# Gate products and whole token-tile splits moved from GpSimd to VectorE at the end of each sub-layer

## Chip, cores and metric

The kernel runs on one core of a Trainium2 chip. The metric is device time in microseconds (us) for one launch. The engines are called PE (TensorE), DVE (VectorE), ACT (ScalarE), POOL (GpSimd) and SP (SyncE, which issues the DMAs).

## What is computed

A trunk of two layers over 256 context tokens and 512 latent tokens of width 1024, in float32. Each layer is a half-step feed-forward block, a token mixer (differential attention in layer 0, grouped-query attention in layer 1), and another half-step feed-forward block. Each of these sub-layers reads a normalised, modulated copy of the residual stream and ends in a gated residual:

```python
def modulated_norm(h, g, m, k):
    return rmsnorm(h, g) * (1.0 + m[..., k + 1, :]) + m[..., k, :]

def gated_residual(h, y, g, m, k, weight):
    return h + weight * m[..., k + 2, :] * rmsnorm(y, g)

# per layer
h = half_ffn(h, m, 0, ...)           # sub-layer s = 0
h = gated_residual(h, mixer(modulated_norm(h, g[2], m, 3)), g[3], m, 3, 1.0)   # s = 1
h = half_ffn(h, m, 6, ...)           # s = 2
```

So between two sub-layers every token tile goes through the same chain: the last partial product of y, the gate product, the mean square of y, the new h, the mean square of h, the normalised h, a transpose, the modulation and a split of the result into a high and a low part for the next sub-layer's matmuls.

## The kernel before

Tokens lie in six tiles of 128 (tiles 0 and 1 context, 2 to 5 latent). Weights and activations are each split into a rounded high part and the remainder, so every product takes three matmuls. The six sub-layers run one after the other; (l, s) below is layer l, sub-layer s. The layer-0 mixer is (0,1), the layer-1 mixer is (1,1), and the other four are feed-forward blocks. The last, (1,2), writes the output and has nothing after it.

In a feed-forward block the output projection is summed over groups of weight rows. In the last group (`w_out_last`) PE goes through the tiles in order, two halves of 512 columns each (`project_half`, matmuls at L423). Each half is added to y by DVE (`add_y`, L414). As soon as both halves of a tile are there the class `Finish` takes the tile through its chain:

- `gated` (L364 to L371, the operation recorded at L369): yg = y * gate for one half of 512 columns, on POOL. The gate rows g were loaded once per sub-layer (`load_gate`, L327). yg is taken from a pool of two buffers in the feed-forward blocks and from the weight buffers wh and wl in the mixers.
- `sumsq` on ACT (L267), then `rms` on POOL, which is two instructions on one column (L97 and L99).
- h = yg * rms + h on DVE (L382, SCALAR_TENSOR_TENSOR over 1024 columns), and a DMA that stores h.
- `sumsq` of h on ACT and `rms` on POOL again, then y = h * rms on DVE (L388, TENSOR_SCALAR over 1024 columns).
- eight transposes on PE into PSUM (`turn`, L280), and the modulation out of PSUM, four blocks on DVE (L294) and four on ACT (L290) in most tiles.
- `split_u`: ACT copies the high part into uh (L310) and the remainder goes into ul. A tile in `WIDE` (thirteen tiles in all: four each at the ends of the sub-layers (0,0), (0,2) and (1,0), one at (0,1)) is split whole: one ACT copy of 1024 columns, then DVE takes the first 512 columns of the remainder (L315) and POOL the other 512 (L316). The other tiles are split in two parts, both remainders on DVE (L318).

Within `w_out_last` of a feed-forward block the order on DVE, ACT and POOL is the program's (a manual schedule). After each half of a tile, the function `stages` advances the tiles that are in flight in the order of stages 3, 4, 5, 1, 2. For DVE that makes, after the first half of a tile t+1: the addition, the modulation of tile t-1, the normalisation (L388) of tile t. After the second half of a tile t: the addition, the remainder of tile t-2, the new h (L382) of tile t. PE's order there, and all orders in the two mixers and at the beginning of the next sub-layer, come from the planner that places instructions by estimated times. The chain of the last two tiles runs on into the next sub-layer, which calls `need(t)` before it uses a tile.

Of the kernel before, what the change touches and what calls it, by code (L numbers as in the profile page):

```python
# [13 lines left out]
ALU = mybir.AluOpType  # L14
# [7 lines left out]
KC = D // P  # L22
# [32 lines left out]
def raw(ap):  # L55
    return ap.bitcast(F32)
# [3 lines left out]
def trunk(ctx: ExitStack, tc: tile.TileContext, a: dict, out: bass.AP):  # L60
    nc = tc.nc
# [85 lines left out]
    marks = {}  # L147
# [155 lines left out]
    def split_u(t, place, parts):  # L303
        i, j = place
        u32 = ys[t].rearrange("p (k q) -> p k q", k=KC)
        n = KC // parts
        for k in range(0, KC, n):
            ks = slice(k, k + n)
            hi, lo = (x[:, i, ks, j * P : (j + 1) * P] for x in (uh, ul))
            marks["act"] = nc.scalar.copy(hi, u32[:, ks])  # L310
            if parts == 1:
                yield
            if parts == 1:
                m = KC // 2
                marks["dve"] = nc.vector.tensor_tensor(out=lo[:, :m], in0=u32[:, :m], in1=raw(hi[:, :m]), op=ALU.subtract)  # L315
                marks["pool"] = nc.gpsimd.tensor_tensor(out=lo[:, m:], in0=u32[:, m:], in1=raw(hi[:, m:]), op=ALU.subtract)  # L316
            else:
                marks["dve"] = nc.vector.tensor_tensor(out=lo, in0=u32[:, ks], in1=raw(hi), op=ALU.subtract)  # L318

    def load_gate(l, s):  # L320
        g = []
# [31 lines left out]
    class Finish:  # L353
# [10 lines left out]
        def gated(self, t, dh):  # L364

            if dh == 0:
                self.yg = self.tile()
            cols = slice(512 * dh, 512 * dh + 512)
            nc.gpsimd.tensor_tensor(  # L369
                out=self.yg[:, cols], in0=ys[t][:, cols], in1=self.gate[1 if t < CT else 0][:, cols], op=ALU.mult  # L370
            )  # L371

        def chain(self, t):
            i, j = self.place[t]
            cols = slice(j * P, (j + 1) * P)
            h = load_h(t, self.first, self.tile if self.s == 1 else None)
            ss = sumsq(ys[t], uh[:, i, :, cols])
            self.gated(t, 1)
            yg = self.yg
            r = rms(ss)  # L380
            yield
            nc.vector.scalar_tensor_tensor(out=h, in0=yg, scalar=r, in1=h, op0=ALU.mult, op1=ALU.add)  # L382
            nc.sync.dma_start(out=hd[t] if self.nxt else out[0, (t - CT) * P : (t - CT + 1) * P], in_=h)
            if not self.nxt:
                return
            r = rms(sumsq(h, ys[t]))
            yield
            nc.vector.tensor_scalar(out=ys[t], in0=h, scalar1=r, scalar2=None, op0=ALU.mult)  # L388
            yield
            pts = turn(t, t in self.wide)  # L390
            modulate(*self.nxt, t, [pts[k // 4][:, (k % 4) * P : (k % 4 + 1) * P] for k in range(KC)])
            yield
            yield from split_u(t, self.place[t], 1 if t in self.wide else 2)
# [1365 lines left out]
```

## Time and profile before

| | |
|---|---|
| median of three runs | 2739.59 us (2735.0 to 2741.33) |
| the profiled execution, whole | 2744.38 us |
| its span, first to last instruction | 2742.6 us |
| granted TensorE clock, mean | 0.988 |
| PE busy | 2639.0 us (96%) |
| DVE busy | 2016.4 us (74%) |
| ACT busy | 1135.7 us (41%) |
| POOL busy | 357.6 us (13%) |

The profile is of one execution. Times are counted from its first instruction. "Busy" is the time between the start and the end of an engine's instructions; consecutive instructions of DVE overlap by some 0.08 us at their ends, so that the spacing of two starts is a little under the duration of the first. A wait is given to the engine whose result came last.

### The profile page before, as it was taken

What the parts mean: (1) busy time and instruction counts of PE and PEld (TensorE: products, weight loads), DVE (VectorE), ACT (ScalarE), POOL (GpSimd) and SP (SyncE); (2) the same over time, 40 slices, a digit from 0 to 9 for tenths busy, and PEclk for the clock granted to TensorE, in tenths of its full rate; (3) what the DMA queues carried; (4) which work ended last, traced back from release to release, by engine and by line L of the source; (5) the groups of instructions that cost most, each with busy time, mean ns of one, the idle gap of its engine ahead of it and who ended that gap; (6) DMA issues with size and microseconds to landing.
All of it is one profiled execution on the core that took longest, in us unless ns stands there. A gap on an engine that the chain in (4) does not pass through costs nothing.

```text
span 2742.6 us, 38868 instructions
## 1 busy us (share of the span) xinstructions
PE 2639.0 (96%) x14720; PEld 2404.6 (88%) x14720; DVE 2016.4 (74%) x3052; ACT 1135.7 (41%) x2323; POOL 357.6 (13%) x643
## 2 busy tenths in 40 slices
PE   6999999989999998999999999999999999899998
PEld 5999998879999987999988789999787899788887
DVE  4988879867777787888788689787766778733355
ACT  4333333156666665333342353333324554622232
POOL 0000000054333343000000310000004210200001
PEclk9999999999999999999999999999999999999999
DMA  7444457531111113444375334344743211444452
GB/s 229 136 132 151 142 170 254 167 122 45 38 32 49 54 63 97 134 124 139 117 251 175 123 104 154 125 137 155 282 141 131 79 39 39 149 142 139 149 166 89
DMA packets 301860, 354.13 MB, mean 129 GB/s; under 512 B 15808, under 2 KB 234088, under 8 KB 301672
## 3 DMA queue, kind: packets, MB, share of 16 engines
q1 hardware_dynamic: 301672, 351.64, 39.9%
q8 instruction: 116, 1.90, 0.3%
q14 instruction: 72, 0.59, 0.1%
HBM read 303.05 MB, written 48.54 MB: 128 GB/s over the span
## 4 chain that ended last, share of the span: by engine, by line
PE 75%; DVE 9%; ACT 5%; issue 5%; POOL 3%; DMA 2%; POOLq 0%; DVEq 0%; ACTq 0%; SPq 0%
PE y_ps L423 23%; PE ff_p L615 15%; PE ff_ps L615 12%; PE ff_ps L735 8%; PE qkv_ps L806 5%; PE ff_ps L477 2%; PE ff_ps L767 1%; DVE h L382 1%; PE S L984 1%; DVE wl L104 1%; PE o_ps L1056 1%; ACT y L267 1%; PE kv_ps L806 1%; PE q_ps L806 1%; PE o_ps L1428 1%
## 5 line engine op out<-in xcount | busy, mean ns | idle before, releaser
L423 PE MATMUL y_ps<-wh,gx 128*128 128x512 f32 x1936 | 604.5, 391 | 1.5 <-ACT wh L103 1.5
L423 PEld LDWEIGHTS y_ps<-wh,gx 128*128 128x128 f32 x1936 | 363.2, 188 | 81.1 <-ACT wh L103 2.9
L103 ACT CAST wh<-stage 128x1024 fp32r<-128x1024 f32 x224 | 232.1, 1048 | 434.7 <-PE y_ps L423 217.0
L423 PE MATMUL y_ps<-wl,gx 128*128 128x512 f32 x968 | 377.3, 390 | 0.5 <-DVE wl L104 0.4
L104 DVE TENSOR_TENSOR wl<-stage,wh 128x1024 fp32r<-128x1024 f32 x224 | 273.2, 1224 | 96.3 <-ACT wh L103 94.4
L414 DVE TENSOR_TENSOR y<-y_ps,y 128x512 f32<-128x512 f32 x324 | 221.3, 686 | 109.3 <-PE y_ps L423 107.7
L369 POOL TENSOR_TENSOR yg<-y,g 128x512 f32<-128x512 f32 x44 | 58.3, 1326 | 1820.3 <-DVE y L414 1818.1
L185 DVE SCALAR_TENSOR_TENSOR acc<-stage,scond,acc 128x1024 f32<-128x1024 f32 x196 | 244.1, 1277 | 30.3 <-DMA stage<-in_ada_w 30.2
L615 PE MATMUL ff_p<-t,wh 128*128 128x384 f32 x960 | 244.4, 335 | 1.5 <-ACT sil L568 1.5
L103 ACT CAST wh<-raw 128x1024 fp32r<-128x1024 f32 x120 | 120.1, 1049 | 255.9 <-DVE raw L594 255.9
L423 PEld LDWEIGHTS y_ps<-wl,gx 128*128 128x128 f32 x968 | 181.8, 188 | 38.5 <-DVE wl L104 1.6
L615 PEld LDWEIGHTS ff_p<-t,wh 128*128 128x128 f32 x960 | 173.8, 188 | 1.8 <-ACT sil L568 1.8
L615 PE MATMUL ff_p<-t,wl 128*128 128x384 f32 x480 | 161.0, 335 | 2.9 <-DVE wl L104 2.9
L615 PE MATMUL ff_ps<-uh,wh 128*128 128x384 f32 x480 | 160.9, 335 | 1.7 <-DVE two L637 1.7
L615 PE MATMUL ff_ps<-uh,wl 128*128 128x384 f32 x480 | 160.4, 334 | 0.0
L615 PE MATMUL ff_ps<-ul,wh 128*128 128x384 f32 x480 | 160.3, 334 | 0.0
L104 DVE TENSOR_TENSOR wl<-raw,wh 128x1024 fp32r<-128x1024 f32 x120 | 141.2, 1218 | 0.0
L806 PE MATMUL qkv_ps<-wh,uh 128*128 128x384 f32 x384 | 136.9, 357 | 4.1 <-ACT wh L849 2.7
L806 PE MATMUL qkv_ps<-wl,uh 128*128 128x384 f32 x384 | 129.8, 338 | 2.5 <-DVE wl L852 2.5
L615 PE MATMUL ff_p<-uh,u 128*128 128x384 f32 x480 | 132.1, 336 | 0.0
L806 PE MATMUL qkv_ps<-wh,ul 128*128 128x384 f32 x384 | 129.9, 338 | 0.1
L615 PE MATMUL ff_ps<-t,wh 128*128 128x384 f32 x480 | 124.6, 340 | 2.2 <-ACT one L633 1.9
(250 smaller groups left out, 6356.4 us busy)
## 6 DMA issues: line engine op xcount, KB each, us to landing
stage<-in_ffn_w_in SPq DMA_DIRECT2D x176, 512.0 KB
stage<-in_ada_w SPq DMA_DIRECT2D x136, 512.0 KB
stage<-in_ffn_w_out SPq DMA_DIRECT2D x88, 512.0 KB
gd<-g SPq DMA_DIRECT2D x66, 384.0 KB
gr<-gd SPq DMA_DIRECT2D x57, 384.0 KB
stage<-in_da_w_in SPq DMA_DIRECT2D x64, 192.0 KB
hd<-h SPq DMA_DIRECT2D x18, 512.0 KB
h<-hd SPq DMA_DIRECT2D x16, 512.0 KB
```

The lines of the kernel that those rows point to most:

```text
L103: nc.scalar.copy(hi, src)
L104: nc.vector.tensor_tensor(out=lo, in0=src, in1=raw(hi), op=ALU.subtract)
L185: nc.vector.scalar_tensor_tensor(out=acc[c], in0=st, scalar=scond[:, k, c : c + 1], in1=acc[c], op0=ALU.mult, op1=ALU.add)
L267: nc.scalar.activation(junk, src, AF.Square, accum_out=ss)
L369: nc.gpsimd.tensor_tensor(out=self.yg[:, cols], in0=ys[t][:, cols], in1=self.gate[1 if t < CT else 0][:, cols], op=ALU.mult)
L382: nc.vector.scalar_tensor_tensor(out=h, in0=yg, scalar=r, in1=h, op0=ALU.mult, op1=ALU.add)
L414: nc.vector.tensor_tensor(out=y, in0=ps, in1=y, op=ALU.add)
L423: nc.tensor.matmul(ps, lhsT=x, rhs=w, start=(i == 0), stop=(i == n - 1))
L477: nc.tensor.matmul(ps, lhsT=ww[:, k, :], rhs=moving(uu, k, two), start=(k == 0 and n == 0), stop=(k == KC - 1 and n == 2),)
L615: nc.tensor.matmul(ps[:, :hw], lhsT=ww[:, k * P : (k + 1) * P], rhs=bb[:, k, cols], start=(first and k == 0 and n == 0), stop=(last and k ...
L735: nc.tensor.matmul(ps[:, :nt], lhsT=ww[:, k, :], rhs=uu[:, :, k, cols], start=(k == 0 and n == 0), stop=(k == KC - 1 and n == 2),)
L806: nc.tensor.matmul(ps[:, :n], lhsT=x, rhs=w, start=(k == 0 and m == 0), stop=(k == KC - 1 and m == 2))
```

## The change

Both edits move work from POOL to DVE. The gate product is issued on DVE at the same place of the program, all 64 of them. The remainder of a whole split is one DVE instruction of 1024 columns in place of two of 512 on two engines. POOL keeps the two one-column instructions of `rms` for each mean square. The dictionary `marks`, which holds the last instructions behind which the next feed-forward block places its first weight loads, no longer gets an entry for POOL from the split; `rms` still sets one.

```diff
@@ split_u
             marks["act"] = nc.scalar.copy(hi, u32[:, ks])
             if parts == 1:
                 yield
-            if parts == 1:
-                m = KC // 2
-                marks["dve"] = nc.vector.tensor_tensor(out=lo[:, :m], in0=u32[:, :m], in1=raw(hi[:, :m]), op=ALU.subtract)
-                marks["pool"] = nc.gpsimd.tensor_tensor(out=lo[:, m:], in0=u32[:, m:], in1=raw(hi[:, m:]), op=ALU.subtract)
-            else:
-                marks["dve"] = nc.vector.tensor_tensor(out=lo, in0=u32[:, ks], in1=raw(hi), op=ALU.subtract)
+            marks["dve"] = nc.vector.tensor_tensor(out=lo, in0=u32[:, ks], in1=raw(hi), op=ALU.subtract)
@@ Finish.gated
             cols = slice(512 * dh, 512 * dh + 512)
-            nc.gpsimd.tensor_tensor(
+            nc.vector.tensor_tensor(
                 out=self.yg[:, cols], in0=ys[t][:, cols], in1=self.gate[1 if t < CT else 0][:, cols], op=ALU.mult
             )
```

## Rows read from the trace of the kernel before

**Rows 1.** Five ends, stretches: busy (count) of PE, PEld, DVE, ACT, POOL; clock; DMA

```profile
540.00:606.00 66.00, 56.37 (x267) 47.85 (x266) 43.95 (x57) 31.33 (x62) 35.30 (x44) 0.95 0.43 139
983.00:1072.00 89.00, 71.11 (x391) 60.34 (x390) 73.51 (x127) 58.45 (x147) 42.23 (x66) 0.90 0.27 90
1538.00:1606.00 68.00, 61.59 (x342) 53.05 (x341) 45.70 (x61) 32.10 (x61) 31.72 (x40) 0.97 0.33 109
2066.00:2136.00 70.00, 60.04 (x305) 51.92 (x304) 47.73 (x65) 31.46 (x63) 36.98 (x46) 0.90 0.45 143
2336.00:2386.00 50.00, 40.48 (x250) 35.38 (x249) 38.23 (x56) 32.63 (x67) 19.50 (x24) 0.93 0.37 123
```

**Rows 2.** PE's waits at the end of (0,2): total us, times, longest

```profile
PE pre_t L280 <- DVE y L388: 2.8, 3, 1.7
PE ff_ps L477 <- ACT y L290: 1.9, 1, 1.9
PE ff_ps L477 <- DVE wl L104: 1.0, 1, 1.0
```

**Rows 3.** PE's waits at the end of (0,0)

```profile
PE qkv_ps L806 <- ACT wh L849: 2.7, 1, 2.7
PE qkv_ps L806 <- DVE wl L852: 2.5, 1, 2.5
PE pre_t L280 <- DVE y L388: 2.3, 2, 1.7
PE k_t L934 <- POOL ks L927: 2.1, 1, 2.1
```

**Rows 4.** PE's waits at the end of (1,0)

```profile
PE k_t L1338 <- DVE xn L1286: 3.2, 1, 3.2
PE kv_ps L806 <- DVE wl L104: 2.6, 1, 2.6
...
PE kv_ps L806 <- ACT wh L103: 1.9, 1, 1.9
```

**Rows 5.** Lines 388, 382, 318: count: shortest/median/longest ns, first and last start

```profile
L388 DVE TENSOR_SCALAR y<-h,rms x18: 753/1758/1775, 551.4 to 2127.9; 128x1024 f32<-128x1024 f32 x18
...
L382 DVE SCALAR_TENSOR_TENSOR h<-yg,rms,h x22: 1279/1794/2316, 547.9 to 2737.6; 128x1024 f32<-128x1024 f32 x22
...
L318 DVE TENSOR_TENSOR ul<-y,uh x30: 676/686/1767, 613.5 to 2382.7; 128x512 fp32r<-128x512 f32 x30
```

**Rows 6.** DVE groups by line, two-input operations: count | busy us, mean ns | idle before

```profile
L104 DVE TENSOR_TENSOR wl<-stage,wh 128x1024 fp32r<-128x1024 f32 x224 | 273.2, 1224 | 96.3 <-ACT wh L103 94.4
...
L509 DVE TENSOR_TENSOR y<-y,y 128x512 f32<-128x512 f32 x9 | 6.2, 688 | 0.2
```

**Rows 7.** DVE's timeline in one turn at (0,2): start, us, instruction, [idle before]

```profile
1562.17 2.32 DVE L382 SCALAR_TENSOR_TENSOR h<-yg,rms,h 128x1024 f32<-128x1024 f32 x1
...
1565.01 1.35 DVE L294 TENSOR_SCALAR y<-pre_t,ab,ab 128x128 f32<-128x128 f32 x4
1566.72 1.77 DVE L388 TENSOR_SCALAR y<-h,rms 128x1024 f32<-128x1024 f32 x1 [0.36 <-POOL rms L99]
1568.42 0.68 DVE L414 TENSOR_TENSOR y<-y_ps,y 128x512 f32<-128x512 f32 x1
1571.26 0.69 DVE L315 TENSOR_TENSOR ul<-y,uh 128x512 fp32r<-128x512 f32 x1 [2.16 <-ACT uh L310]
```

**Rows 8.** POOL's timeline in the same turn

```profile
1561.60 1.80 POOL L316 TENSOR_TENSOR ul<-y,uh 128x512 fp32r<-128x512 f32 x1
...
1566.66 1.30 POOL L369 TENSOR_TENSOR yg<-y,g 128x512 f32<-128x512 f32 x1
```

**Rows 9.** POOL's timeline at the end of (0,1), two products together

```profile
1057.27 2.98 POOL L369 TENSOR_TENSOR wh<-y,g 128x512 f32<-128x512 f32 x2 [0.27 <-DVE y L414]
```

**Rows 10.** Line 1078 within 985 to 1072 us, the end of (0,1), columns as before

```profile
L1078 DVE TENSOR_SCALAR o<-o,rs x8: 274/906/1306, 984.5 to 1050.4; 128x128 f32<-128x128 f32 x8
```

**Rows 11.** DVE's timeline, last tile of the program

```profile
2737.65 1.29 DVE L382 SCALAR_TENSOR_TENSOR h<-yg,rms,h 128x1024 f32<-128x1024 f32 x1 [2.24 <-POOL rms L99]
```

## The prediction

> **What bounds the kernel now.** I read the busy shares first: PE is at 96% of the span, so only stretches in which PE waits can give anything back. Those that this change touches are the six ends of sub-layers, and the table by stretch shows the five that have a successor [rows 1]. The reader is to see three things there. PE's clock is below its mean of 0.988 in each: 0.95, 0.90, 0.97, 0.90 and 0.93 of full speed. DVE is busy 44 to 48 us out of 66 to 70 at the three feed-forward ends that have a successor, and 73.5 of 89 us at the end of (0,1). POOL is busy only 13% of the whole span, but 32 to 42 us at each of the first four ends, so it works there and almost nowhere else.
>
> Next I read PE's waits at those ends. They sum to 6.3 us at (0,2) (the three rows and 0.6 us in two smaller ones) [rows 2], 9.6 us at (0,0) [rows 3] and 10.0 us at (1,0), where the row for L388 reads as it does at (0,0) [rows 3, 4]. The wait for L388 recurs, and the others name weight splits that stand behind L388 and the modulation in DVE's or ACT's queue. So the late thing is the serial loop DVE, ACT, POOL that takes a tile through its chain.
>
> The timeline of one turn of this loop shows why [rows 7, 8]. A turn lasts 9.69 us, from the new h (L382) at 1562.17 to the next one at 1571.26 + 0.60 = 1571.86. The two DVE instructions that are long in it are long while POOL works on SBUF: L382 takes 2.32 us beside the POOL half of a split (1561.60, 1.80 us), and L388 takes 1.77 us beside a gate product (1566.66, 1.30 us). The same two instructions take 1.28 and 0.75 us at their shortest [rows 5]. Each ends about when the POOL instruction ends plus its own short duration (1563.40 + 1.28 against 1564.49 measured in the first case). The addition L414, which reads PSUM and one SBUF tile, keeps 0.68 us [rows 7]. So POOL's wide instructions hold DVE up, and this is a loss of 1.03 + 1.00 us in a turn.
>
> **The change, part by part: a feed-forward end.** I go through the turn with the new order, by spacing of starts. Old: L382 and the addition to 1565.01 (2.84 us), the modulation with an idle 0.36 to 1566.72 (1.71), L388 to 1568.42 (1.70), the addition and the wait for ACT's high part to 1571.26 (2.84), the half split (0.60). That is 9.69.
>
> New: L382 without the collision 2.24 - 1.03 = 1.21. The addition 0.69, since the product now reads its result straight away. The product, a two-input DVE operation of 512 columns, 0.69 by its duration and 0.61 by spacing [rows 6]. The modulation 1.35. L388 can thus start 1.21 + 0.69 + 0.61 + 1.35 = 3.86 us into the turn. The mean square of h allows it from 4.55 - 1.03 = 3.52, so 0.34 us of the added product shows here. L388 without its collision takes 1.70 - 1.00 = 0.70. Then the addition; the second product (0.69) lies wholly inside the 2.16 us in which DVE waits for ACT's high part [rows 7], so it costs nothing, and would cost 0.61 if that wait were gone. That part stays 2.84. The whole split takes 1.22 instead of 0.69 [rows 6], so 1.14 by spacing. Sum: 3.86 + 0.70 + 2.84 + 1.14 = 8.54, against 9.69: 1.15 us less in each turn.
>
> The turns that this shortens are those of tiles 2 to 5 (in the first two the loop still waits for PE's halves), so the last tile's L382 starts 4 x 1.15 = 4.6 us sooner and, since its own collision goes as well, ends 5.6 us sooner. The splits of the first weights, the last normalisation and the last modulation follow it. PE can give back 6.3, 9.6 and 10.0 us of waits at these three ends, so it can take the 5.6. I take **5.5 us at each of (0,0), (0,2) and (1,0), together 16.5**. The bounds for one end: at the low end of the gain only the waits for L388, 2.3 to 2.8 us; at the high end the chain's 5.6 and the half-speed time. PE's lost clock in the five stretches is worth (1 - clock) x length = 3.3 + 8.9 + 2.0 + 7.0 + 3.5 = 24.7 us [rows 1]; it falls behind the waits, so part of it may go with them. I take none of it in the sum and 8 us, a third, in the range.
>
> DMAs: no transfer is added. The gate buffers are freed when the last product is done, which is sooner, and the next weight loads wait for such buffers on SP's queue. The gates are loaded well before the first product at each end, so DVE does not come to wait for a DMA in POOL's place. The yg buffer of a tile is freed by an L382 that stands earlier in the same DVE queue.
>
> **The end of (0,1).** DVE gets 12 products of 0.69 and half of one split, 0.53: 8.8 us. It loses the collisions of L1078, which takes 0.27 us at its shortest and 1.31 at its longest there; with a median of 0.91 about half of the eight are long, so 4 x 1.03 [rows 10]. Three others stand beside them: 1.1 on the whole split, 1.1 on one L318 and 0.65 on one L388 [rows 5], together 6.9. That is 1.9 us more work on an engine that is idle 15.5 of 89 us [rows 1]. Against it, POOL's queue is freed: two products issued together hold it 2.98 us, with the mean square of the same tile queued behind them [rows 9]. On DVE they stand between the additions, and the mean square waits for ACT alone. The bounds are +8.8 (all additions on the path) and -6.9 (all collisions on the path). I take -1, near the middle, because the work almost balances.
>
> **The end of (1,1).** Eight products, 5.5 us, on a DVE that is busy 38 of 50 us [rows 1], against the same kind of collisions. Bounds +5.5 and -3; I take -1 by the same balance.
>
> **The end of (1,2).** The last tile's L382 waits for the mean square [rows 11]. The product fits in the 2.24 us in which DVE idles ahead of it, and POOL's product ended with ACT's sum, so nothing moves: 0, bounds +0.2 and -0.2.
>
> Sum against the profiled execution: 2744.4 - 16.5 - 1 - 1 = 2725.9. The profiled execution lies 4.8 us above the median of the three runs, so the median to expect is **2721**.
>
> **The rivals.**
>
> *Something else is late next* (17%). The planner orders the first instructions of the next sub-layer, and a weight split, or the DMA of the lambda rows at (0,0) that waits for a freed h buffer, may take the place of the chain. Then only the waits for L388 go: 2.3 + 2.8 + 2.3 = 7.4 us, which gives 2737.0 profiled and 2732 in the median. For it: three of PE's four waits at (0,0) and at (1,0) are not for L388. Against it: what they wait for stands behind L388 in the same queues.
>
> *The mixers' ends take it back* (8%). If DVE sets the pace at (0,1) and (1,1), the additions cost up to 8.8 + 5.5 = 14.3, and 16.5 - 14.3 leaves 2.2: 2737, no change. It decides if the 15.5 idle us at (0,1) are spread in pieces too short for a product. For it: DVE is 83% busy there. Against it: the collisions removed are nearly as long as the products added. The Trainium skill ("Perfetto Trace Analysis", Optimizing Scalar/DVE Operations) says that with a saturated DVE it may pay to offload to ScalarE or even GpSimd, and warns that the shared port can spoil the latter; the first half speaks against this change, the second for it. By the first half alone the two ends would cost the 14.3.
>
> *GpSimd's one-column instructions are held up by DVE* (6%, slower). The two instructions of `rms` stand on the loop twice in a turn. If a DVE product is running when they are due, and holds them as POOL's products held DVE, each pair waits up to 0.69: 1.38 a turn, more than the 1.15 gained, so 0.23 x 12 turns = 3 us lost, and with the mixers' 14.3 the median is 2757. The Trainium skill ("SBUF — State Buffer", Who interferes with whom) states that a DVE instruction with two SBUF inputs and a GpSimd instruction that reads SBUF block each other, and that whichever starts first runs to its end. The collisions of L382 and of the split agree with it; that the roles change is what this rival takes from it. It decides where a product starts less than 0.69 us ahead of an `rms`. Against it: in the new turn the first product ends at 1.21 + 0.69 + 0.69 = 2.59 us, just when the mean square of h is out of ACT, and the modulation that runs next reads PSUM; the second product ends 1.4 us after its addition began, while ACT's sum is still running.
>
> *The collisions are not POOL's* (3%, slower). If L382 and L388 stay at 2.3 and 1.8 us, a turn grows by 0.34 and 0.54, 0.88 x 12 = 10.6 us, median about 2750. The short L388 where POOL is idle speaks against it [rows 5].
>
> **How the numbers follow.** The forecast has the remaining 66%. A measurement of this kernel can tell about 0.2%, 5.5 us, from no change. Faster by more than that are the forecast and the first rival, 0.83; within it the second, 0.08; slower the last two, 0.09. The range goes down to 2721 - 8 (clock) - 2 (more collisions on the path in the mixers) = 2711, and up past the first rival to 2735; it leaves out the last three rivals, 17%.
>
> **What would show it.** In the profile of the changed kernel L388 and L382 should be near 0.75 and 1.28 us throughout, POOL should have nothing longer than 1 us at the ends, and the turn at (0,2) should be near 8.5 us. PE should no longer wait for L388 at the feed-forward ends, and the last L382 of (0,2) should lie some 5 us nearer to the first half of its group. I am wrong if the turn is shorter but the next sub-layer's first matmuls stay where they were, if one-column POOL instructions grow beyond 0.6 us, or if PE's waits at (0,1) grow by more than 5 us.

## The result, and the profile after

The changed kernel takes 2724.5 us (median of 6 runs, 2722.6 to 2726.2) against 2739.9 us (6 runs, 2735.0 to 2742.3): a ratio of 0.9942, 95% interval 0.9931 to 0.9952. That is 15.4 us less; 18.6 had been forecast. The profiled execution took 2722.7 us, with a span of 2720.9. Behind the edit the line numbers are 5 lower: L382 is now L377, L388 is L383, L414 is L409, L369 is L364, and L313 is the remainder of every split.

**The turn.** DVE's timeline in one turn at the end of (0,2): start, duration in us, engine, line, instruction, and in brackets the idle time ahead with what ended it.

```profile
1552.29 1.28 DVE L377 SCALAR_TENSOR_TENSOR h<-yg,rms,h 128x1024 f32<-128x1024 f32 x1
1553.48 0.68 DVE L409 TENSOR_TENSOR y<-y_ps,y 128x512 f32<-128x512 f32 x1
1554.20 0.69 DVE L364 TENSOR_TENSOR yg<-y,g 128x512 f32<-128x512 f32 x1
1554.81 1.36 DVE L294 TENSOR_SCALAR y<-pre_t,ab,ab 128x128 f32<-128x128 f32 x4
1556.09 0.74 DVE L383 TENSOR_SCALAR y<-h,rms 128x1024 f32<-128x1024 f32 x1
1556.75 0.68 DVE L409 TENSOR_TENSOR y<-y_ps,y 128x512 f32<-128x512 f32 x1
1557.47 0.69 DVE L364 TENSOR_TENSOR yg<-y,g 128x512 f32<-128x512 f32 x1
1559.78 1.23 DVE L313 TENSOR_TENSOR ul<-y,uh 128x1024 fp32r<-128x1024 f32 x1 [1.62 <-ACT uh L310]
1560.92 1.28 DVE L377 SCALAR_TENSOR_TENSOR h<-yg,rms,h 128x1024 f32<-128x1024 f32 x1
```

The turn, from one L377 to the next, is 1560.92 - 1552.29 = 8.63 us (8.64 in the next one); it was 9.69 [rows 7]. The new h takes 1.28 us where it took 2.32, and the normalisation 0.74 where it took 1.77. The added product ahead of the modulation leaves no idle time ahead of the normalisation (it was 0.36), the second one eats into the wait for ACT (1.62 instead of 2.16 us), and the whole split takes 1.23 instead of 0.69.

The same over the whole kernel, the lines by themselves: shortest, median and longest duration in ns, first and last start, shapes.

```profile
L377 DVE SCALAR_TENSOR_TENSOR h<-yg,rms,h x22: 1277/1284/1286, 545.0 to 2716.0; 128x1024 f32<-128x1024 f32 x22
L383 DVE TENSOR_SCALAR y<-h,rms x18: 742/747/754, 548.5 to 2105.2; 128x1024 f32<-128x1024 f32 x18
L364 DVE TENSOR_TENSOR yg<-y,g x44: 681/692/694, 539.4 to 2713.8; 128x512 f32<-128x512 f32 x44
```

Median and longest are now the shortest of before (1284 for 1794 and 2316, 747 for 1758 and 1775 [rows 5]): no instruction of these lines is held up any more.

**The ends.** The table by stretch of the same five ends, each moved along with its work: busy us (count) of PE, PEld, DVE, ACT, POOL, then granted clock, DMA share, GB/s.

```profile
537.00:598.00 61.00, 55.84 (x270) 47.86 (x269) 44.16 (x69) 30.82 (x62) 13.68 (x28) 0.97 0.46 150
975.00:1064.00 89.00, 72.05 (x400) 62.21 (x398) 73.32 (x135) 58.37 (x144) 26.98 (x53) 0.88 0.27 89
1529.00:1591.00 62.00, 59.78 (x344) 51.92 (x343) 46.88 (x73) 31.78 (x61) 10.02 (x24) 1.00 0.36 120
2050.00:2112.00 62.00, 55.57 (x296) 48.33 (x295) 46.74 (x76) 29.62 (x60) 15.31 (x30) 0.95 0.48 157
2312.00:2364.00 52.00, 40.88 (x247) 36.23 (x246) 41.21 (x64) 32.63 (x67) 8.17 (x16) 0.90 0.38 120
```

Against [rows 1] the three feed-forward ends (first, third, fourth line) are shorter, with a higher clock: 0.97, 1.00 and 0.95 for 0.95, 0.97 and 0.90. The stretches don't hold quite the same matmuls (296 for 305 in the fourth line), so they are compared over the same work further down. The two mixers' ends (second and fifth line) are not shorter, and their clock is lower: 0.88 and 0.90 for 0.90 and 0.93. DVE's busy time did not grow at (0,1), 73.3 us for 73.5, though 12 products were added. POOL works 10 to 15 us where it worked 32 to 37.

PE's waits at the ends of (0,0), (0,2) and (1,0): total us, times, longest.

```profile
PE k_t L929 <- POOL ks L922: 4.1, 1, 4.1
PE qkv_ps L801 <- DVE wl L847: 1.1, 2, 0.6
```

```profile
PE pre_t L280 <- DVE y L383: 1.8, 2, 1.1
PE ff_ps L472 <- DVE ul L313: 0.2, 1, 0.2
PE ff_ps L472 <- ACT uh L310: 0.2, 1, 0.2
```

```profile
PE k_t L1333 <- DVE xn L1281: 6.3, 1, 6.3
```

At (0,0) 5.2 us are left of 9.6 [rows 3], at (0,2) 2.2 of 6.3 [rows 2], at (1,0) 6.5 within the stretch of the table, of 10.0 [rows 4]. At (0,0) and (1,0) the weight splits are no longer what PE waits for, or hardly; one wait for the first k_t of the mixer has grown (2.1 to 4.1 and 3.2 to 6.3), which fits PE's getting there sooner.

To say what each end gave, I took in both traces the time between the same two pieces of work, one ahead of the end and one behind it (at a feed-forward end, from a late store of the hidden block to a fixed matmul of the next sub-layer; at a mixer, from its last input projection to an early store of the next block). In us, after minus before:

| | (0,0) | (0,1) | (0,2) | (1,0) | (1,1) | (1,2) | sum |
|---|---|---|---|---|---|---|---|
| forecast | -5.5 | -1 | -5.5 | -5.5 | -1 | 0 | -18.5 |
| the changed kernel | -5.5 | +0.4 | -6.3 | -7.7 | +2.3 | 0.0 | -16.8 |

The rest of the difference between the two profiled executions (21.7 us) lies in stretches that the change doesn't touch, 2.9 us of it ahead of the last group of (0,0), so a single entry of the table is good to about 1 to 2 us.

### The profile page after: what moved, and what is told of

It is laid out like the page before. It is cut to its first block, busy times and chain, and to the rows that moved or that the text cites. A ratio compares the mean times of both kernels' runs of the same rounds, so it can differ in the third digit from the quotient of the medians.

```text
span 2720.9 us, 38900 instructions
## 1 busy us (share of the span) xinstructions
PE 2632.6 (97%) x14720; PEld 2402.3 (88%) x14720; DVE 2026.2 (74%) x3116; ACT 1135.2 (42%) x2323; POOL 255.6 (9%) x566
## 4 chain that ended last, share of the span: by engine, by line
issue 75%; PE 16%; POOL 3%; DVE 3%; ACT 2%; DMA 0%; POOLq 0%; DVEq 0%; ACTq 0%
PE qkv_ps L801 6%; PE y_ps L418 3%; POOL rms L99 1%; PE S L979 1%; PE o_ps L1051 1%; PE kv_ps L801 1%; PE q_ps L801 1%; PE o_ps L1423 1%; POOL ms L97 1%; ACT e L999 1%; PE S L1379 1%; POOL rs L91 1%; PE p_t L1031 1%; PE p_t L1403 0%; PE o_ps L1058 0%
## 5 line engine op out<-in xcount | busy, mean ns | idle before, releaser
L409 DVE TENSOR_TENSOR y<-y_ps,y 128x512 f32<-128x512 f32 x324 | 222.0, 688 | 101.4 <-PE y_ps L418 99.6
L97 POOL TENSOR_SCALAR ms<-ss 128x1 f32<-128x1 f32 x66 | 23.5, 356 | 2045.7 <-ACT uh L267 1918.0
```

Source lines behind the costliest of these rows:

```text
L97: nc.gpsimd.tensor_scalar(out=ms, in0=ss, scalar1=D * EPS, scalar2=None, op0=ALU.add)
L409: nc.vector.tensor_tensor(out=y, in0=ps, in1=y, op=ALU.add)
```

## Experiments

The theory: POOL's wide instructions held DVE's up, the loop of a tile is shorter by what they cost, and the feed-forward ends take the gain. The rivals: the gain comes from POOL's queue (the mean square no longer waits behind wide work), or the mixers' ends give part of it back. In the expectations the theory is the one of the port, the first rival the one of the queue. All edits are against the changed kernel.

**One half at a time.** First the split as it was, the products staying on DVE:

```diff
+            if parts == 1:
+                m = KC // 2
+                marks["dve"] = nc.vector.tensor_tensor(out=lo[:, :m], ...)
+                marks["pool"] = nc.gpsimd.tensor_tensor(out=lo[:, m:], ...)
```

> Only the gate products go to DVE; a whole split stays half on DVE, half on POOL. Port theory (a POOL instruction of 512 columns holds up the DVE instruction beside it, inside a serial loop): L388's collision goes (0.75 us), L382's stays (2.3 us). By the steps of the prediction a turn is 4.89 + 0.70 + 2.84 + 0.60 = 9.03 us, against 9.69 before and 8.63 with both edits, and the three feed-forward ends give back 3 x 4 x 0.66 = 8 us. The two mixers' ends lose the 2.7 us that they lose with both edits, if the products are the reason. Ratio to before 0.998. Queue theory (the gain is that the two one-column instructions of rms no longer stand behind wide work in POOL's queue): the products are 64 of 77 wide instructions and stand right ahead of rms, so nearly the whole gain is here, ratio 0.995.

Then the products back on POOL, the split staying whole:

```diff
-            nc.vector.tensor_tensor(
+            nc.gpsimd.tensor_tensor(
                 out=self.yg[:, cols], in0=ys[t][:, cols], ...
```

> Only the whole split goes to DVE; the products stay on POOL. Port theory: L382 is short (1.28 us), L388 keeps its collision (1.76 us). A turn is 3.52 + 1.70 + 2.84 + 1.14 = 9.20 us, against 9.69 before; each feed-forward end gives back 4 x 0.49 + 1.03 = 3 us, together 9, and the mixers' ends move less than 1 us. Ratio to before 0.9967. Queue theory: the splits stand behind rms, not ahead of it, so almost nothing is gained, and the longer DVE split costs 0.53 a turn, ratio 1.000 to 1.002.

Measured: the first 2730.5 us, 0.9962 (0.9950 to 0.9975), with a turn of 9.13 us; the second 2731.6 us, 0.9965 (0.9951 to 0.9978), with a turn of 9.19. DVE's and POOL's timeline of the first, then of the second:

```profile
1559.56 2.32 DVE L382 SCALAR_TENSOR_TENSOR h<-yg,rms,h 128x1024 f32<-128x1024 f32 x1
1564.40 0.74 DVE L388 TENSOR_SCALAR y<-h,rms 128x1024 f32<-128x1024 f32 x1
...
1559.00 1.80 POOL L316 TENSOR_TENSOR ul<-y,uh 128x512 fp32r<-128x512 f32 x1
```

```profile
1557.59 1.28 DVE L377 SCALAR_TENSOR_TENSOR h<-yg,rms,h 128x1024 f32<-128x1024 f32 x1
1561.12 1.77 DVE L383 TENSOR_SCALAR y<-h,rms 128x1024 f32<-128x1024 f32 x1 [0.36 <-POOL rms L99]
...
1561.05 1.29 POOL L364 TENSOR_TENSOR yg<-y,g 128x512 f32<-128x512 f32 x1
```

With POOL's half of the split the new h takes 2.32 us and the normalisation 0.74; with POOL's product it is the other way round. Each collision stands where its POOL instruction is and nowhere else. The two halves take 0.56 and 0.50 us off the turn, together the 1.06 of both. The second run also speaks against POOL's queue as the cause: the products, behind which the mean squares stand, are all on POOL there as before, yet the kernel is 9 us faster, where the queue theory expected a ratio of 1.000 to 1.002.

The time of the first run was missed: 0.998 had been expected, and the kernel is 4.8 us faster than that. Its feed-forward ends gave 3.3, 4.1 and 5.3 us, 12.7 instead of 8. The queue theory's 0.995 lies at the end of the interval, so that this time doesn't decide between the two; the rows above and the second run do.

**The mixers.** The products of the two mixers go back to POOL, those of the feed-forward ends stay on DVE:

```diff
-            nc.vector.tensor_tensor(
+            (nc.gpsimd if self.s == 1 else nc.vector).tensor_tensor(
```

> As after the change, but the products at the two mixers' ends (20 of 64) stay on POOL. In the profile after the change the ends of (0,1) and (1,1) lose 0.4 and 2.4 us. If the products on DVE are the cause, these 2.7 us come back and the feed-forward ends keep their gain: about 2722, ratio to before 0.9933. If instead the planner's order at (1,1) changes by chance with anything before it, the loss stays or changes sign, ratio 0.992 to 0.995.

2720.4 us, 0.9926 (0.9913 to 0.9938): 4 us better than the full change. The three feed-forward ends are the same (-5.7, -6.3, -8.4); (0,1) gives -1.9 instead of +0.4 and (1,1) +0.8 instead of +2.3. The intervals of this ratio and of the full change's overlap a little, but the run after next says the same. The time alone also fits the expectation's second reading (0.992 to 0.995), and two single traces don't tell which of the two ends gives the gain; all the traces together do. Taken between two matmuls of PE on either side, seven kernels whose mixers are those of the changed one came out between -2.1 and +0.9 us at (0,1) and between +1.3 and +3.9 at (1,1); the three with these products on POOL came out between -2.4 and -0.2, and between +0.1 and +0.9. So at (1,1) the products are better left on POOL, by some 2 us. At (0,1) the two groups overlap, and a loss through the products is not shown there.

**One product for two.** A single product of 1024 columns behind a tile's second half, at the feed-forward ends:

```diff
-            if dh == 0:
+            if self.s != 1 and dh == 0:
+                return
+            if dh == 0 or self.s != 1:
...
-            cols = slice(512 * dh, 512 * dh + 512)
+            cols = slice(512 * dh if self.s == 1 else 0, 512 * dh + 512)
```

> As after the change, but at the feed-forward ends the two products of a tile are one DVE instruction of 1024 columns after the second addition, where DVE waits for ACT's high part. By the steps of the prediction the product ahead of the modulation showed 0.34 us of a turn; without it L388 waits for rms again and a turn is 3.52 + 0.70 + 2.84 + 1.14 = 8.20 us against 8.63. Four turns at three ends: 5 us, of which the end of (0,2) can give only about 2 (PE waits 2.2 us there after the change), so 3 to 4 us: 2721, ratio to before 0.993. If the loop is not what sets these ends any more, no change against after: 0.9942.

The turn is 8.23 us, 0.4 less, since nothing is added ahead of the modulation any more. The time is 2723.1 us, 0.9937 (0.9924 to 0.9949): 1.4 us better by the medians, which the intervals can't tell from nothing. The ends were -6.7, -7.1 and -7.8, 1.2, 0.9 and 0.1 more than in the changed kernel; twelve turns at 0.4 would have been 4.9. A shorter loop pays less here, which fits PE's waits at these ends being partly used up: 2.2 us in all are left at (0,2) above.

**Both of these together.**

> The two versions that were faster than the change, together: products of the mixers' ends on POOL, and one DVE product of 1024 columns per tile at the feed-forward ends, whole splits on DVE. If their gains add: 2724.5 - 4.1 - 1.5 = 2719, ratio to before 0.992. If the gain of one came from the same waits as the other's, 2720.5, ratio 0.9926. Turn at the feed-forward ends 8.23 us.

2719.9 us, 0.9928 (0.9915 to 0.9940), with turns of 8.23 and 8.50 us. The median is nearer to the second reading, but the interval holds both, so whether the gains add isn't shown. It is the fastest of the kernels here, by an amount over the run with the mixers' products on POOL alone (2720.4) that can't be told from nothing. The three kernels with the mixers' products on DVE (the changed one, the one above and the next) have 2724.5, 2723.1 and 2723.4; the two with them on POOL 2720.4 and 2719.9.

**The order at (1,1).** In the timeline of the changed kernel the row maximum (L1384) stands behind the new h, which waits 0.77 us for its mean square; in the kernel before, the row maximum (there L1389) stood ahead of the new h. First the changed kernel, then the one before:

```profile
2317.76 1.28 DVE L377 SCALAR_TENSOR_TENSOR wl<-wh,rms,wl 128x1024 f32<-128x1024 f32 x1 [0.77 <-POOL rms L99]
2318.96 0.95 DVE L1384 TENSOR_REDUCE neg<-S 128x1 f32<-128x768 f32 x1
```

```profile
2340.27 0.95 DVE L1389 TENSOR_REDUCE neg<-S 128x1 f32<-128x768 f32 x1
2341.73 1.28 DVE L382 SCALAR_TENSOR_TENSOR wl<-wh,rms,wl 128x1024 f32<-128x1024 f32 x1 [0.51 <-POOL rms L99]
```

The experiment puts the scores one place ahead in the order of kinds that the planner of this mixer is given:

```diff
-GA_SLOT_END = "PpLFSxHVJCjGYE"
+GA_SLOT_END = "PpLSFxHVJCjGYE"
```

> As after the change, but in the last slots of the grouped-attention mixer the next scores with their row maximum come ahead of the new h in program order. In the profile after the change the end of (1,1) lost 2.3 us, and there the row maximum (L1384) stands behind the new h (L377), which waits 0.77 us for rms; in the profile before, it stood ahead of it. If that order is the cause, the 2.3 us come back: 2722, ratio to before 0.9934. If it is the work of the products itself (8 x 0.69 us on a busy DVE), nothing changes: 0.9942.

2723.4 us, 0.9938 (0.9925 to 0.9952), and (1,1) at +1.0 instead of +2.3. PE's wait behind the row maximum, 3.6 us in the changed kernel, is 1.7 here, but its waits for the normalisation rose from 3.8 to 4.8. The direction fits, but with +1.3 to +3.9 in the kernels that have the same mixers +1.0 is too little to call it shown. In the kernel with all products on POOL as before the end of (1,1) came out at +0.9, not at zero, so its +2.3 may not be all the product's.

**POOL's work put back without use.** A product on POOL whose result nobody reads, at the place of the first product, 400 and then 200 columns, measures the collision by itself:

```diff
+            if self.s != 1 and dh == 0:
+                c2 = slice(0, 400)
+                nc.gpsimd.tensor_tensor(out=self.spent[:, c2], in0=ys[t][:, c2], ...)
...
+        fin.spent = xp.tile([P, 400], F32, name="spent")
```

> As after the change, plus an idle POOL product of 400 columns per tile (gate times the first half of y into a tile that nobody reads) at the place of the first gate product of the feed-forward ends. It adds work to an engine that is nearly idle and takes none from any other. Port theory: in POOL's queue it follows the rms of h, so it starts at 1555.8 in the turn of the profile after the change and runs 1.30 x 400/512 = 1.0 us, to 1556.8; L383 is due at 1556.09 and is held until then. L383 grows from 0.75 to about 1.5 us, the turn from 8.63 to 9.4, and three ends of four turns lose 9 us: 2733, ratio to before 0.9975. Theory that the moved work only had to leave POOL's queue ahead of rms: the added product stands behind rms and costs nothing; turn 8.63, ratio 0.994.

> The same with 200 columns (0.5 us). Port theory with waiting until the other's end: the product ends at 1556.3, L383 is held about 0.2 us, not half of what 400 columns cost; turn 8.85, three ends lose 3 us: 2727, ratio 0.9955. If the two engines shared bandwidth instead of one waiting for the other's end, the cost would go with the columns, half of the cost of 400: turn 9.0, ratio 0.996.

Measured: 2740.3 us, 1.0000 (0.9991 to 1.0009), with turns of 8.95; and 2734.3 us, 0.9981 (0.9972 to 0.9990), with turns of 8.64, the changed kernel's own. Both expectations were missed twice: the turns grew less than expected, and the time grew far more than the turns. The normalisation in the two runs, DVE's row and POOL's, 400 columns first:

```profile
1553.78 1.25 DVE L388 TENSOR_SCALAR y<-h,rms 128x1024 f32<-128x1024 f32 x1
...
1553.43 1.05 POOL L369 TENSOR_TENSOR spent<-y,g 128x400 f32<-128x400 f32 x1
```

```profile
1554.44 0.81 DVE L388 TENSOR_SCALAR y<-h,rms 128x1024 f32<-128x1024 f32 x1
...
1554.09 0.62 POOL L369 TENSOR_TENSOR spent<-y,g 128x200 f32<-128x200 f32 x1
```

What DVE loses is what is left of POOL's instruction when DVE's begins, less 0.2 us: 1554.48 - 1553.78 = 0.70 left and 1.25 - 0.75 = 0.50 lost; 0.27 left and 0.06 lost; in the kernel before 1.24 left and 1.02 lost [rows 7, 8]. So it waits for the other's end and then runs at its own speed. The expectation had this wait: it put 0.71 us of POOL's 400 columns behind the start of the normalisation, and 0.70 were found. It missed the 0.2 us, and it missed that the turn grew by 0.31 us where the normalisation lost 0.50: ACT's sum of y now began 0.03 us behind the addition that it waits for, and in the changed kernel 0.22 us, since ACT was still at its own modulation there.

That leaves 9.8 us that the 200 columns cost without a longer turn. The cause showed in a place where the chain plays no part, the whole of (1,2): 2.1 us longer in both runs. There PE's matmuls of the output projection came further apart. The unused tile of 1600 bytes is laid out ahead of the other tiles of its pool, and moves them, some of the gx among them, which these matmuls load as weights. The next three runs take the two suspects apart.

**Place or port.** The same products into a tile of 384 columns (1536 bytes), which still moves the tiles behind it but by another amount; and the tile of 400 columns with one column written:

```diff
-        fin.spent = xp.tile([P, 400], F32, name="spent")
+        fin.spent = xp.tile([P, 384], F32, name="spent")
```

```diff
-                c2 = slice(0, 200)
+                c2 = slice(0, 1)
```

> The 200-column product on GpSimd of the earlier run, with its unused result in a tile of 384 columns (1536 bytes) instead of 400 (1600 bytes). In the two earlier runs the projection's matmuls L423 came every 230.8 ns on average, in the changed kernel every 227.0 ns; 2840 of them make 10.8 us. The place theory says that the 1600-byte tile shifted the tiles behind it, among them gx that these matmuls load, and that this, not GpSimd, cost most of the 9.8 us: here the pace is 227 ns again, the end of (1,2) is 0.0 against before instead of +2.1, and the median is 2723.5, ratio 0.994. The port theory says that GpSimd's product costs the 9.8 us: 2734, ratio 0.998, pace 231 ns.

> The long product on GpSimd, 384 columns in place of 400, in a tile of 384 columns. Place theory: pace 227 ns, so the 10.8 us go, and what GpSimd's product itself costs stays: turns 8.95 us as with 400 columns, four shortened turns at each of three ends lose 0.3 us each, 4 us in all; 2729.5, ratio 0.996. Port theory: 2740, ratio 1.000.

> The changed kernel with the 400-column tile, and a GpSimd product of one column into it in place of 200 or 400. Place theory: pace 230.8 ns, turns 8.64 us, 2724.5 + 10.8 = 2735, ratio 0.998. Port theory: one column costs GpSimd next to nothing, so the time is the changed kernel's, 2724.5, ratio 0.994, pace 227 ns.

| tile, columns on POOL | us | ratio (95%) | turn | gx matmuls every |
|---|---|---|---|---|
| none (the changed kernel) | 2724.5 | 0.9942 (0.9931 to 0.9952) | 8.64 | 227.0 ns |
| 384, 200 | 2726.8 | 0.9949 (0.9934 to 0.9964) | 8.64 | 227.1 ns |
| 384, 384 | 2728.5 | 0.9956 (0.9941 to 0.9970) | 8.91 | 227.1 ns |
| 400, 1 | 2733.3 | 0.9973 (0.9963 to 0.9982) | 8.64 | 230.8 ns |
| 400, 200 | 2734.3 | 0.9981 (0.9972 to 0.9990) | 8.64 | 230.8 ns |
| 400, 400 | 2740.3 | 1.0000 (0.9991 to 1.0009) | 8.95 | 230.8 ns |

Most of the time goes with the tile, not with POOL's columns: one column into the 400-column tile costs 8.8 us, 200 columns into the other one 2.3. In the groups by line the matmuls read as follows (count, busy us, mean ns), within the first 80 us of the last output projection. First the changed kernel, then the one with one column:

```profile
L418 PE MATMUL y_ps<-wh,gx 128*128 128x512 f32 x213 | 66.0, 390 | 0.0
L418 PE MATMUL y_ps<-wl,gx 128*128 128x512 f32 x106 | 41.2, 389 | 0.0
```

```profile
L423 PE MATMUL y_ps<-wh,gx 128*128 128x512 f32 x229 | 71.8, 393 | 0.0
L423 PE MATMUL y_ps<-wl,gx 128*128 128x512 f32 x115 | 45.3, 394 | 0.0
```

3 to 5 ns a matmul, some 2900 of which make the 9 to 11 us. That it is the place of gx can be seen within one run. Of the 22 gx operands of a block, ten (4 to 7, 12 to 15, 20 and 21) lie in the pool of the unused tile, the others in a pool that this tile doesn't move. In the groups with unmoved operands alone (0 to 2 and 9 to 11) the matmuls come every 227.2 to 227.3 ns in all six kernels of the table. In the group with moved ones alone (12 to 14) they come every 226.7 ns in the first three and every 233.3 ns in the last three. The place theory holds, with 8.8 us where 10.8 was expected. What POOL's 384 columns cost is then 4.0 us by the medians (2728.5 - 2724.5; the intervals of the two ratios overlap), of which 0.27 us in each of twelve turns explain 3.2; for the 200 columns 2.3 us lie within the intervals. In the tile of 400 columns the step from 200 to 400 costs 6.0 us, of which 0.31 us in each of twelve turns explain 3.7; the rest is open. Which alignment gx needs was not tried.

## Why the prediction was right, and where its terms were off

**What bounds the kernel, and the collisions: right.** L377 and L383 take 1.28 and 0.75 us throughout, and each half of the change removes the collision that the prediction gave to it. The rival that the collisions are not POOL's is out.

**The turn: right.** 8.63 us against 8.54. The four terms measure 3.80 + 0.66 + 3.03 + 1.14 for 3.86 + 0.70 + 2.84 + 1.14. The first product shows as 0.28 us (0.34 forecast): the normalisation starts 3.80 us into the turn, and 3.52 us in the run with one product. The second lies in the wait for ACT, as forecast. The term that is off is the 2.84, the way from the second addition to the split: ACT's modulation starts at 1556.27 and takes 1.51 us, so that ACT's sum of y begins 0.22 us behind the addition, where it was 0.03.

**The feed-forward ends: 16.5 us forecast, 19.5 measured.** The chain came out as forecast: counted from the first matmul of the last group, the last new h ends 6.0, 5.4 and 5.2 us sooner at (0,0), (0,2) and (1,0), for 5.6. What PE made of it did not. The following rows hold the same matmuls in both kernels (to one at the edges), from the first of the last group to a fixed one of the next sub-layer, at (0,0), (0,2) and (1,0), first before, then after (columns as in [rows 1]):

```profile
537.86:669.69 131.83, 119.87 (x665) 108.44 (x664) 87.86 (x150) 70.27 (x186) 62.26 (x103) 0.97 0.28 86
1535.41:1627.15 91.74, 85.33 (x481) 76.36 (x480) 69.10 (x97) 45.05 (x83) 31.72 (x40) 0.98 0.33 108
2063.62:2179.33 115.71, 103.00 (x633) 92.99 (x632) 83.90 (x168) 56.68 (x145) 49.87 (x68) 0.94 0.34 107
```

```profile
534.97:661.35 126.38, 118.94 (x666) 108.08 (x664) 88.02 (x162) 69.79 (x186) 40.57 (x87) 0.99 0.29 90
1526.60:1612.07 85.47, 83.25 (x481) 75.00 (x480) 70.01 (x109) 44.63 (x83) 10.02 (x24) 1.00 0.36 116
2047.23:2155.37 108.14, 99.81 (x633) 90.68 (x632) 83.84 (x180) 56.13 (x145) 27.99 (x52) 0.97 0.35 114
```

PE's idle time (length less busy) fell by 4.5, 4.2 and 4.4 us, together 13.1, where the prediction has 16.5. Its busy time for the same matmuls fell by 0.9, 2.1 and 3.2, together 6.2, where the sum has nothing. Both make 19.3. In these stretches the clock stood at half speed (1.2 GHz) for 6.8, 3.4 and 13.7 us before, and for 3.4, 0 and 6.8 us after. Half of the difference, 6.8 us, is about what the busy time gave. So two terms were off, and in opposite directions: PE took less of the chain's 5.6 us than it was given, because it then waits for something else (next paragraph), and a third of the gain came back as clock, most at (1,0). The prediction had the clock in its range (8 us), not in its sum. All this is read from one execution of each kernel; over the whole kernel the granted clock is 0.988 to 0.989 in the six executions after the change and 0.986 to 0.991 in those of the kernel before, so the third holds for these ends in these two traces and not for the whole kernel.

**Something else is late next: half right.** At (0,0) and (1,0) PE does end up waiting for something new, the first k_t of the mixer, 4.1 and 6.3 us. The rival expected the gain to be lost by that; it wasn't, the new wait only took over what was left. At (1,0) the run with one product shows that this limit is near: a turn shorter by 0.4 us gives 0.1 us there. At (0,2) PE still waits for the normalisation, 1.8 us of 2.8, where the prediction had said that it should not.

**The mixers' ends: wrong in sign.** Forecast -1 and -1, measured +0.4 and +2.3, together 4.7 us worse. Moving the products back to POOL there gave 4 us in the medians. By the kernels with the same mixers the loss is real at (1,1), and the +0.4 at (0,1) can't be told from -1. The step that failed is "by the same balance" at (1,1): the middle of the bounds given there, +5.5 and -3, is +1.25, and -1 has the other sign; at (0,1), with +8.8 and -6.9, the middle is +0.95. At (0,1) the balance of work holds (DVE busy 73.3 us for 73.5), but equal busy time is not equal lateness. PE's waits went from 17.5 to 16.7 us at (0,1) and from 9.4 to 11.3 at (1,1), and the clock's loss, (1 - clock) x length, rose by 10.7 - 8.9 = 1.8 and 5.2 - 3.5 = 1.7. The added products stand between additions, score work and weight splits whose order the planner fixes, and in (1,1) that order changed too; what of the loss there is the product and what the order isn't settled. The rival that put both ends at 14.3 us was far too high.

**GpSimd's one-column instructions: the event is there, its price is small.** The groups by line have the two instructions of `rms` at a mean of 356 and 611 ns for 325 and 596 before, over 66 each: 3 us in all, spread over the kernel. In the turn above they take 0.22 and 0.57 us as before; the product ends ahead of them, as the prediction worked out. But by the prediction's sign, beyond 0.6 us, the event is there at some tiles, as it was before: the longest L97 is 2.88 us, at the last tile of (1,0), where 1.19 was the longest before (rows in the last section).

**The end of (1,2): right.** 0.0 us in the changed kernel.

The total is 15.4 instead of 18.6: 3.0 more than forecast at the feed-forward ends, 4.7 less at the mixers', and 1.5 less for the difference between one profiled execution and the medians. These errors partly cancel, so that the total came this near to the forecast is in part luck.

## What to carry to other kernels

Before work is moved off an engine, look at what it does to the other engine's instructions that overlap it: a short form of the same instruction elsewhere in the trace gives the loss directly. Moving the work wins this loss back where the receiving engine has waits to hide the work in, as at the feed-forward ends; at the end of (1,1) it cost some 2 us. Add the clock's share to the sum where a stretch with waits is below full clock: here it was a third of the gain. And when an experiment allocates a tile, compare the pace of untouched instructions first, since moving other tiles can cost more than what is tested.

## What was not expected of the hardware

**Where gx lies sets PE's pace.** With a 1600-byte tile ahead of some of the gx, the matmuls that load the moved ones came every 233.3 ns instead of 226.7, with a tile of 1536 bytes every 226.7, and the matmuls of the unmoved groups every 227.2 in all of them. Over all gx that is 230.8 for 227.0, and over the kernel 8.8 us.

**The hold goes both ways, and is a wait for the end.** In the run with one column POOL's unused product takes 190 ns in the median, and where it begins just behind DVE's product it takes as long as DVE's 0.69 us (the line by itself, then all engines' timeline):

```profile
L369 POOL TENSOR_TENSOR spent<-y,g x22: 185/190/696, 543.8 to 2723.7; 128x1 f32<-128x1 f32 x22
```

```profile
2716.76 0.69 DVE L364 TENSOR_TENSOR yg<-y,g 128x512 f32<-128x512 f32 x1
2716.80 0.70 POOL L369 TENSOR_TENSOR spent<-y,g 128x1 f32<-128x1 f32 x1 [2.00 <-DVE y L414]
```

In the pairs shown so far the one that started first went through, and DVE's instructions came free some 0.2 us sooner than POOL's recorded end. The Trainium skill ("SBUF — State Buffer", Who interferes with whom) describes it as an exclusive lock in which the one that issues first keeps the shared ports for its whole instruction; the three pairs of left and lost time above agree with that.

The order of starts does not decide every case. At the last tile of (1,0) in the changed kernel, L97 began inside the first of two weight splits, and it ended only behind the second and behind a whole split, both of which began after it (POOL's timeline, then DVE's):

```profile
2098.03 2.88 POOL L97 TENSOR_SCALAR ms<-ss 128x1 f32<-128x1 f32 x1 [3.52 <-ACT uh L267]
```

```profile
2097.34 2.35 DVE L104 TENSOR_TENSOR wl<-stage,wh 128x1024 fp32r<-128x1024 f32 x2
2099.61 1.22 DVE L313 TENSOR_TENSOR ul<-y,uh 128x1024 fp32r<-128x1024 f32 x1
```

It ended at 2100.91, 0.08 us behind the last of the three (2100.83); the three follow each other without a gap. What decides who goes next there was not tried.

The same section of the Trainium skill also says that PE never waits on anyone, and no run here shows PE held up by POOL: its slower pace came with the tile's place (230.8 ns with one column on POOL, 227.1 with 384).
